# Output projection of a hybrid encoder layer: seven half-size products in two passes instead of one full product, on one Trainium2 core

## The chip, the cores and the metric

The kernel runs on one core of one Trainium2 chip. The metric is the device time in microseconds of one execution; the median of a few runs is compared. A profiled execution of the same program gives the trace from which all rows below come. In those rows PE is TensorE (the matrix engine) and PEld its weight loads, DVE is VectorE, ACT is ScalarE, POOL is GpSimd, SP is SyncE, which only issues DMAs here.

## The reference

One layer on 512 tokens of width 1024, all in float32. Two branches mix the tokens and a gated FFN follows:

```python
h = rmsnorm(x, mix_norm)
p = h @ w_in                                   # 1024 x 9248
rx, ry, qkv, z, ba, gates = split(p)
y_rnn = rglru_branch(rx, ry, ...) @ w_rnn_proj # 1536 x 1024
y_dn = deltanet_branch(qkv, z, ba, ...) @ w_dn_proj
g_rnn, g_dn = split(sigmoid(gates))
x = x + (g_rnn * y_rnn + g_dn * y_dn) @ w_out  # 1024 x 1024: the output projection
h = rmsnorm(x, ffn_norm)
gt, up = split(h @ w_gate_up)                  # 1024 x 5632
x = x + (silu(gt) * up) @ w_down               # 2816 x 1024
return rmsnorm(x, final_norm)
```

DeltaNet has 8 heads of width 128, worked on here as four pairs of heads.

## The kernel before, in words

**Matmuls in three terms.** Float32 operands are split into a rounded part (`hi`) and the rest (`lo = raw - f(hi)`). Each product is `hi*hi + hi*lo + lo*hi`, three matmuls. ScalarE makes `hi` (a cast), VectorE makes `lo` (a subtraction); `parts_of`, `split` and `stage` do this.

**Weights.** SP loads them block by block into a ring of four buffers `wraw` of 128 x 1024 floats; a buffer is free again when ScalarE and VectorE have split it. `stage` and `weights` put the parts into `whi` and `wlo`, others into tiles of the pools `t2` (128 x 512) and `t4` (128 x 1024), which all show as `t` in the profile.

**Order.** The program is first recorded: each operation goes into a list with its engine, the tiles it touches, a cost and a due time. `Plan.order()` then lays out one order for each engine from costs, due times and the free buffers, and that order is what is built; at run time each engine, and SP's queue too, takes its instructions strictly in that order and waits for semaphores. `spend(us)` opens a new recording stage, and the table `TIMES` gives each stage the due time at which its operations are sorted. All instructions are issued in one helper, so the rows all have line L384; tiles tell them apart.

**Stages.** First norm; the RG-LRU branch and the input projection; then the four head pairs `g` of DeltaNet: `dn_mats`, `dn_inverse` (a triangular inverse by small dependent steps on VectorE), `dn_state` and `dn_out`, with input projections and gates between them that keep TensorE at work. Then `dn_part(h0, nh, n)` does DeltaNet's projection for column block `n` over `nh` heads, first heads 0 to 5 and then 6 and 7, and adds the gated result to `mixs`, the mixed sum, transposed (features on partitions, tokens along the free dimension), as four tiles of two feature blocks.

**Output projection (`out_mm`).** `mixs` is split into `mh`. The 512 tokens are four blocks `c` of 128, kept as rows `x1[c]` (in the tile `na`). For the first half of the columns the four weight blocks `k2` (256 rows x 512 columns) are run over all four `c`, into four PSUM banks; for the second half each `c` is done alone with all weights ready (`weights_w`). Each `c` is added to `x1[c]`, squared, scaled by its norm, and, two blocks at a time, transposed and split by `norm_split` into `hh2` and `hl2`, first the tokens 0 to 255, then 256 to 511. The unsplit transposes stay in `a1` (tokens 0 to 255) and `a2`.

**Gate/up and down.** Two tiles `n` are done plainly (`gate_up_plain`), by token halves through `mm3`. The other twenty already use seven products for eight on blocks 2 x 2 (`gate_up`): VectorE forms four sums of the weights, and the combinations `q5`, `q7`, `q6`, `q3` of `a1` and `a2` are made once. `m` is the first combination that VectorE reads from the `st` bank of a tile. The down projection does the same in two passes; its weight sums are made ahead by `down_sums` (two additions on VectorE for each of eleven blocks, stored to DRAM as `sums`), which stands behind the last split of `mixs`.

Of the kernel before, what the change touches and what calls it, by code (L numbers as in the profile page):

```python
# [14 lines left out]
P = 128  # L15
# [39 lines left out]
LASTK = 3  # L55
GATES = (0, 2, 4, 6, 16)
# [333 lines left out]
def trunk(ctx: ExitStack, tc: tile.TileContext, x, mix_norm, w_in, rg_conv_w, rg_conv_b, rg_wa, rg_ba, rg_wx, rg_bx,  # L390
# [789 lines left out]

    gates = [(rnn_gate, n) for n in range(KD)] + [(dn_gate, n) for n in range(KD)]
    for g in range(4):
        spend()
        dn_mats(g)
        spend()
        dn_inverse(g)
        spend()
        dn_state(g)
        if g < 3:
            dn_z(g)  # L1190
        spend()
        dn_out(g)
        if g < 3:
            dn_front(g + 1)
        if g == 2:
            dn_z(3)
        for fn, n in gates[GATES[g]:GATES[g + 1]]:
            fn(n)
    spend()
    for h in range(6):  # L1200
        dn_split(h)
    for n in range(KD):
        dn_part(0, 6, n)
    spend()
    for h in (6, 7):
        dn_split(h)
    mh = []
    for n in range(KD):
        dn_part(6, 2, n)
        y = four(F32R)  # L1210
        split(mixs[n // 2][:, n % 2, :], y)
        mh.append(y)
# [10 lines left out]
    scaled = {}  # L1223

    def norm_split(c0, whole):


        sc = [scaled[c] for c in (c0, c0 + 1)]
        for k2 in range(KD // 2):
            pt = axb()  # L1230
# [11 lines left out]
    def weights_w(src):  # L1242
        now = plan.t
        raw = new(wp, (P, 2, 512), "wraw", NW)
        hi = four(F32R)
        lo = four(F32R)
        plan.t = now - 20
        Q.dma_start(raw, src)
        plan.t = now - AHEAD
        A.copy(hi, raw)  # L1250
        V.tensor_tensor(lo, raw, f(hi), ALU.subtract)
        plan.t = now
        return hi, lo

    wo = w_out[0].rearrange("(k p) n -> p k n", p=P)
    hh2 = new(hp, (P, KD, S), "hh", 1, F32R)
    hl2 = new(hp, (P, KD, S), "hl", 1, F32R)
    def out_mm(po, c, k2, hi, lo):
        spend(1.3)
        cs_ = slice(c * P, (c + 1) * P)  # L1260
        for k in (2 * k2, 2 * k2 + 1):
            T.matmul(po, mh[k][:, 0, cs_], hi[:, k % 2, :], start=k == 0, stop=False)
            T.matmul(po, mh[k][:, 0, cs_], lo[:, k % 2, :], start=False, stop=False)
            T.matmul(po, mh[k][:, 1, cs_], hi[:, k % 2, :], start=False, stop=k == KD - 1)

    def wo_part(k2, half):
        return wo[:, 2 * k2:2 * k2 + 2, half * 512:(half + 1) * 512]
# [6 lines left out]
    ssh = []  # L1274
    for c in range(NT):
        V.tensor_tensor(x1[c][:, 0:512], pos[c], x1[c][:, 0:512], ALU.add)
        sa = small([P, 1], "ssq", 4)
        A.activation(two(), x1[c][:, 0:512], AF.Square, accum_out=sa)
        sb = small([P, 1], "ssh", 4)
        V.tensor_scalar(sb, sa, 1.0 / D, EPS, ALU.mult, ALU.add)  # L1280
        ssh.append(sb)
    ws = [weights_w(wo_part(k2, 1)) for k2 in range(4)]
    a1 = [four(shape=(P, 4, 256)) for _ in range(2)]
    a2 = [four(shape=(P, 4, 256)) for _ in range(2)]
    for c in range(NT):
        po = mmb()
        for k2 in range(4):
            out_mm(po, c, k2, *ws[k2])
        V.tensor_tensor(x1[c][:, 512:D], po, x1[c][:, 512:D], ALU.add)
        plan.t -= 10  # L1290
        scaled[c] = four(shape=(P, D))
        ssq, rst, rin = (small([P, 1], t, 4) for t in ("ssq", "rst", "rin"))
        V.scalar_tensor_tensor(two(), x1[c][:, 512:D], 1.0, x1[c][:, 512:D], ALU.mult, ALU.mult, accum_out=ssq)
        act(rst, ssq, AF.Sqrt, scale=1.0 / D, bias=ssh[c])
        V.reciprocal(rin, rst)
        V.tensor_scalar(scaled[c], x1[c], rin, None, ALU.mult)
        plan.t += 10
        if c % 2:
            norm_split(c - 1, a1 if c == 1 else a2)

# [13 lines left out]
    def gate_up_plain(n):  # L1314
        pos = []
        for c0 in (n * P, D_FF + n * P):
# [3 lines left out]
            mm3(po, hi, lo, lambda k: hh2[:, k, :], lambda k: hl2[:, k, :], KD, 2)  # L1320
# [3 lines left out]
        for h in range(2):  # L1324
# [304 lines left out]
```

## Time and profile before

| | |
|---|---|
| median of three runs | 1057.54 us (1056.54 to 1057.62) |
| the profiled execution | 1057.59 us, its span in the trace 1055.8 us |
| TensorE's granted clock, mean | 0.998 |
| instructions | 17690 |
| bytes moved by DMA | 122.83 MB |

The page gives, for each engine, its busy time, the share of the span and the count; for the chain that ended last, the share of each engine; and groups of instructions as `out<-in shapes xcount | busy us, mean ns of one | idle before`. A table of stages has one row for each stretch of the span: its length, then the busy time and the count of each engine, the granted clock, the mean busy share of the 16 DMA engines and GB/s. A row of the timeline has start, duration, engine, operation, and in brackets the idle time just before with what ended it.

### The profile page before, as it was taken

How to read it: one execution, taken by the hardware profiler on the slowest of the kernel's cores; microseconds unless marked ns; L12 is line 12 of the kernel's file. 1: busy time of each engine (PE TensorE's matmuls, PEld its weight loads, DVE VectorE, ACT ScalarE, POOL GpSimd, SP SyncE). 2: the span in 40 equal slices, each digit the busy share in tenths (PEclk: the TensorE clock that was granted, in tenths of full speed). 3: DMA queues.
4: the chain of work that ended last, by engine and by line, in shares of the span. 5: the costliest groups of instructions: out<-in, count | busy, mean ns of one | idle time of the engine just before them, and what ended most of it. 6: DMA issues, size and time to landing. Idle time of an engine off the chain costs nothing.

```text
span 1055.8 us, 17690 instructions
## 1 busy us (share of the span) xinstructions
PE 1042.7 (99%) x6731; PEld 909.3 (86%) x6731; DVE 868.2 (82%) x1606; ACT 676.9 (64%) x1245; POOL 61.4 (6%) x109
## 2 busy tenths in 40 slices
PE   8999999999999999999999999999999999999997
PEld 7888888888888888888888798789999999998886
DVE  7669999659895797489479558879999988889997
ACT  7799989596538678675766643447554453546664
POOL 2000000105100321000020000000000000000000
PEclk9999999999999999999999999999999999999999
DMA  9422232224441243313202223875554333336532
GB/s 271 110 70 80 81 95 75 85 80 125 117 118 52 58 117 100 91 43 98 72 25 78 79 71 123 300 238 177 170 183 148 101 105 96 100 115 214 192 119 80
DMA packets 174389, 122.83 MB, mean 116 GB/s; under 512 B 5952, under 2 KB 160720, under 8 KB 174304
## 3 DMA queue, kind: packets, MB, share of 16 engines
q1 hardware_dynamic: 172832, 118.41, 37.3%
q10 hardware_dynamic: 1184, 3.15, 0.8%
q8 instruction: 53, 0.87, 0.3%
q14 instruction: 32, 0.26, 0.1%
q0 software_dynamic: 288, 0.13, 0.1%
HBM read 113.78 MB, written 7.90 MB: 115 GB/s over the span
## 4 chain that ended last, share of the span: by engine, by line
PE 96%; DMA 1%; ACT 1%; DVE 1%; issue 0%; ACTq 0%; SPq 0%; DVEq 0%
PE mm L384 57%; PE ax L384 24%; PE st L384 15%; ACT t L384 1%; DMA wraw<-in_w_in_dram 1%; DMA wraw<-in_w_out_dram 1%; DVE na L384 0%; DVE t L384 0%; DVE wlo L384 0%; ACTq L384 0%; ACT L384 0%; ACT rst L384 0%; SPq L384 0%; ACT hh L384 0%; DVE hl L384 0%
## 5 line engine op out<-in xcount | busy, mean ns | idle before, releaser
L384 DVE TENSOR_TENSOR t<-t,t 128x512 fp32r<-128x512 f32 (+22 forms) x489 | 242.9, 506 | 29.6 <-ACT t L384 18.5
L384 PE MATMUL mm<-hh,whi 128*128 128x512 f32 (+2 forms) x648 | 228.8, 363 | 0.0
L384 PE MATMUL mm<-hl,whi 128*128 128x512 f32 (+2 forms) x648 | 228.4, 362 | 0.0
L384 ACT CAST whi<-wraw 128x1024 fp32r<-128x1024 f32 (+3 forms) x139 | 130.1, 937 | 128.4 <-PE mm L384 60.5
L384 DVE TENSOR_TENSOR wlo<-wraw,whi 128x1024 fp32r<-128x1024 f32 (+3 forms) x138 | 151.3, 1096 | 59.4 <-ACT whi L384 29.3
L384 PE MATMUL mm<-hh,wlo 128*128 128x512 f32 (+1 forms) x632 | 146.6, 364 | 0.0
L384 PE MATMUL ax<-t,t 32*32 32x32 f32 (+3 forms) x1062 | 138.4, 285 | 0.3 <-issue 0.3
L384 PEld LDWEIGHTS mm<-hh,whi 128*128 128x128 f32 (+1 forms) x648 | 121.6, 188 | 17.0
L384 PEld LDWEIGHTS mm<-hl,whi 128*128 128x128 f32 (+1 forms) x648 | 121.6, 188 | 16.9
L384 ACT CAST t<-t 128x512 fp32r<-128x512 f32 (+2 forms) x140 | 88.7, 650 | 56.0 <-DVE t L384 50.7
L384 PEld LDWEIGHTS ax<-t,t 128*128 128x128 f32 (+1 forms) x1062 | 109.6, 159 | 17.4 <-issue 2.1
L384 PEld LDWEIGHTS mm<-hh,wlo 128*128 128x128 f32 x632 | 108.6, 189 | 17.3 <-issue 0.2
L384 ACT ACT_TABLE_LOAD x70 | 89.8, 1283 | 4.8 <-PEq L1615 1.7
L384 DVE SCALAR_TENSOR_TENSOR t<-mm,par,t 128x511 f32<-128x511 f32 (+1 forms) x108 | 80.0, 742 | 13.0 <-ACT t L384 11.9
L384 PE MATMUL mm<-t,t 128*128 128x256 f32 (+1 forms) x468 | 89.9, 336 | 0.0
L384 PE MATMUL mm<-t,whi 128*128 128x512 f32 x320 | 81.7, 395 | 0.0
L384 PEld LDWEIGHTS mm<-t,t 128*128 128x128 f32 x468 | 72.8, 190 | 8.9 <-DVE t L384 0.2
L384 PEld LDWEIGHTS mm<-t,whi 128*128 128x128 f32 x320 | 59.3, 188 | 12.4 <-ACT whi L384 0.4
L384 ACT CAST t<-wraw 128x1024 fp32r<-128x1024 f32 (+1 forms) x51 | 44.6, 880 | 26.3 <-DMA wraw<-in_w_gate_up_dram 8.8
L384 ACT ACTIVATE t<-t 128x128 f32<-128x128 f32 (+4 forms) x86 | 46.9, 558 | 22.4 <-DVE t L384 20.9
L384 DVE TENSOR_TENSOR t<-wraw,t 128x1024 fp32r<-128x1024 f32 (+1 forms) x51 | 51.2, 1006 | 2.5 <-ACT t L384 2.4
L384 POOL TENSOR_SCALAR_AFFINE_SELECT t<-t 128x512 f32<-128x512 f32 x32 | 33.1, 1042 | 163.9 <-DMA t<-gcr 103.2
(206 smaller groups left out, 1695.0 us busy)
## 6 DMA issues: line engine op xcount, KB each, us to landing
wraw<-in_w_in_dram SPq DMA_DIRECT2D x72, 512.0 KB, 3.7
wraw<-in_w_gate_up_dram SPq DMA_DIRECT2D x44, 512.0 KB, 3.8
wraw<-in_w_rnn_proj_dram SPq DMA_DIRECT2D x16, 384.0 KB, 3.4
t<-in_w_down_dram SPq DMA_DIRECT2D x11, 512.0 KB, 7.3
sums<-t SPq DMA_DIRECT2D x11, 512.0 KB, 4.4
wraw<-sums SPq DMA_DIRECT2D x11, 512.0 KB, 3.2
wraw<-in_w_down_dram SPq DMA_DIRECT2D x22, 256.0 KB, 3.8
wraw<-in_w_down_dram SPq DMA_DIRECT2D x11, 512.0 KB, 3.6
```

The costliest lines, as they stand in the source:

```text
L384: self.plan.add(e, lambda: real(*a, **kw), outs, ins, cost, tail, table)
```

## The change

The output projection `Y = X W` is done by blocks 2 x 2: tokens in halves (the two pairs of blocks `c`), features and columns in halves. Seven products of half-size blocks, named "1" to "7", take the place of eight; each contracts over 512 features as four pairs of 128-blocks `j`. The scheme is the one that gate/up and down have.

- *Weight sums* (`out_sums`): after the second head pair (`g == 1`) is recorded, four blocks `j` of `w_out` are loaded, two buffers of `wraw` each, four additions of 512 columns make the sums, and they are stored to DRAM as `osums`.
- *DeltaNet's projection* is cut 4 and 4 heads instead of 6 and 2 (`DSPLIT`).
- *Token combinations* (`out_q`, `out_q2`): made from `mixs` as its tiles are completed; the second set is made while the first pass runs.
- *First pass*: products "6", "7", "5", "1" for both token blocks `i`, into eight PSUM banks, `j` by `j`. Then `m` is formed and added to three quarters of `x1`.
- *Second pass*: "4" goes on in the bank of "7", "2" in that of "1", "3" in that of "5". "4" completes the tokens 256 to 511, whose norm is then done first; "2" and "3" complete the tokens 0 to 255.
- `gate_up_plain` runs the second token half first. Part of the squares and of the scaling moves from VectorE to ScalarE, and half of `norm_split`'s transposes use the `st` banks.
- `TIMES` is another table throughout.

```diff
+DSPLIT = 4
-    def mm3(po, hi, lo, xh, xl, kk, parts=1):
+    def mm3(po, hi, lo, xh, xl, kk, parts=1, last_first=False):
-        for t in range(0, S, n):
+        for t in range(0, S, n)[::-1 if last_first else 1]:
...
+    wo = w_out[0].rearrange("(j h p) n -> p j h n", p=P, h=2)
+    def out_sums(j):
+        ra, rb, s_ = new(wp, (P, 2, 512), "wraw", NW), new(wp, (P, 2, 512), "wraw", NW), four()
+        Q.dma_start(ra, wo[:, j, 0, :].rearrange("p (h n) -> p h n", h=2))
+        Q.dma_start(rb, wo[:, j, 1, :].rearrange("p (h n) -> p h n", h=2))
+        V.tensor_tensor(s_[:, 0, :], ra[:, 0, :], ra[:, 1, :], ALU.add)
+        V.tensor_tensor(s_[:, 1, :], ra[:, 1, :], rb[:, 1, :], ALU.add)
+        V.tensor_tensor(rb[:, 1, :], s_[:, 0, :], rb[:, 1, :], ALU.add)
+        V.tensor_tensor(rb[:, 0, :], rb[:, 1, :], rb[:, 0, :], ALU.add)
+        Q.dma_start(osums[j][:, 0], s_)
+        Q.dma_start(osums[j][:, 1], rb)
...
-    for h in range(6):
+    for h in range(DSPLIT):
         dn_split(h)
     for n in range(KD):
-        dn_part(0, 6, n)
+        dn_part(0, DSPLIT, n)
...
+    def out_q(j):
+        mj = mixs[j].rearrange("p h (s t) -> p (h s) t", s=2)
+        q = two(shape=(P, 2, 256))
+        V.tensor_tensor(q, mj[:, 0:2, :], mj[:, 1:4:2, :], ALU.subtract)
+        V.tensor_tensor(mj[:, 1, :], mj[:, 0, :], q[:, 1, :], ALU.subtract)
+        (p1, p6), (p7, p5) = pair(mj[:, 0:2, :], 2), pair(q, 2)
+    def out_q2(j):
+        V.tensor_tensor(mj[:, 1, :], mj[:, 2, :], mj[:, 1, :], ALU.subtract)
+        p3, p2, p4 = pair(mj[:, 1:4, :], 3)
...
-    pos = [stb(), stb(), axb(), axb()]
-    for k2 in range(4):
-        hi, lo = stage(lambda raw: [(raw, wo_part(k2, 0))], (P, 2, 512))
-        for c in range(NT):
-            out_mm(pos[c], c, k2, hi, lo)
+    def out_w(j):
+        Q.dma_start(ra[:, 0, :], wo[:, j, 0, 0:512])
+        Q.dma_start(ra[:, 1, :], osums[j][:, 1, 1, :])
+        Q.dma_start(rs, osums[j][:, 0])
+        (w1, w6), (w5, w7) = halves(ra, True), halves(rs)
+    def out_w2(j):
+        Q.dma_start(r, wo[:, j, 1, :].rearrange("p (h n) -> p h n", h=2))
+        Q.dma_start(t4_, osums[j][:, 1, 0, :])
+        w2, w3 = halves(r)
+        parts_of(t4_, th, tl, 0)
+    ob = {"6": [stb(), stb()], "7": [axb(), axb()], "5": [axb(), mmb()], "1": [mmb(), mmb()]}
+    for j in range(nj):
+        spend(5.5)
+        w4 = out_w(j)
+        for name in "6751":
+            for i in range(2):
+                half_mm(ob[name][i], i, w4[name], xq[j][name], j == 0, j == nj - 1)
+        out_q2(j)
...
+    for i in range(2):
+        V.tensor_tensor(hi_[:, 512:D], hi_[:, 512:D], ob["7"][i], ALU.subtract)
+        V.tensor_tensor(hi_[:, 512:D], hi_[:, 512:D], ob["5"][i], ALU.add)
+        V.tensor_tensor(m, ob["6"][i], m, ALU.subtract)
+        V.tensor_tensor(hi_[:, 0:512], hi_[:, 0:512], m, ALU.subtract)
+        V.tensor_tensor(hi_[:, 512:D], hi_[:, 512:D], m, ALU.add)
+        V.tensor_tensor(lo_[:, 512:D], lo_[:, 512:D], m, ALU.add)
...
+    for j in range(nj):
+        w3s.append(out_w2(j))
+    def out_last(name, bank, i):
+        for j in range(nj):
+            half_mm(ob[bank][i], i, w3s[j][name], xq[j][name], False, j == nj - 1, True)
+    for i in range(2):
+        out_last("4", "7", i)
+        sc.append(scale_chunk(2 + i, 0, False))
+    norm_split(2, sc, a2)
+    for i in range(2):
+        out_last("2", "1", i)
+    for i in range(2):
+        out_last("3", "5", i)
+        sc.append(scale_chunk(i, 512, True))
+    norm_split(0, sc, a1)
...
 TIMES = [
-    -193727, -159384, -193730, -126073, -120235, -159028, -125968, -63810, -13198, -66391, -64154, -63637, -49334,
+    -176998, -159417, -176656, -106634, -96501, -159195, -96162, -70221, 191167, -94063, -87550, -69365, -34065,
```

What the new order is at three places. TensorE, in the middle of the output projection. Before, at the turn from the first half of the columns to the second: `st_1137` is the bank of the last token block of the first half, `mm_1186` that of the second block of the second half.

```order
L384 MATMUL st_1137<-whi_1150,t_1129 128x512
L384 MATMUL st_1137<-wlo_1151,t_1129 128x512
...
L384 MATMUL mm_1186<-t_1165,t_1087 128x512
L384 MATMUL mm_1186<-t_1166,t_1087 128x512
...
L384 MATMUL mm_1186<-t_1165,t_1093 128x512
L384 MATMUL mm_1186<-t_1166,t_1093 128x512
```

Now, at the turn from the first pass to the second: `mm_1171` is a bank of "1", `ax_1168` one of "5" (product "3" goes on in it), `ax_1166` the bank of "7" for `i = 0`, in which "4" goes on; `t_1178`, `t_1186` and `t_1194` are the combinations of `out_q2` for `j` = 0, 1 and 2.

```order
L384 MATMUL mm_1171<-whi_1198,t_1154 128x512
L384 MATMUL mm_1171<-wlo_1199,t_1154 128x512
L384 MATMUL ax_1168<-t_1218,t_1178 128x512
L384 MATMUL ax_1168<-t_1219,t_1178 128x512
L384 MATMUL ax_1168<-t_1218,t_1179 128x512
L384 MATMUL mm_1171<-whi_1198,t_1155 128x512
L384 MATMUL ax_1166<-t_1220,t_1178 128x512
L384 MATMUL ax_1166<-t_1221,t_1178 128x512
L384 MATMUL ax_1166<-t_1220,t_1179 128x512
L384 MATMUL ax_1166<-t_1226,t_1186 128x512
```

What moved: a matmul of product "3" already stands among the last ones of the first pass, and the second pass begins with "4", whose weight sums come from `osums`.

VectorE, in the second half of the same stage. Before, around the additions of the first half (`na` is `x1`); `t_1317`, `t_1341` and `t_1366` are blocks of `down_sums`, `wlo_1215` and `wlo_1219` weights of the first plain gate/up tile.

```order
L384 TENSOR_TENSOR t_1317<-t_1317 128x512
L384 TENSOR_TENSOR na_1130<-mm_1180,na_1130 128x512
L384 TENSOR_TENSOR na_1130<-ax_1139,na_1130 128x512
...
L384 TENSOR_TENSOR wlo_1215<-wraw_1213,whi_1214 128x1024
...
L384 TENSOR_TENSOR t_1341<-t_1341 128x512
L384 TENSOR_TENSOR wlo_1219<-wraw_1217,whi_1218 128x1024
...
L384 TENSOR_TENSOR t_1366<-t_1366 128x512
```

Now, around the splits of the second pass's weights: `t_1225`, `t_1231` and `t_1237` are the `lo` parts for products "2" and "3" of `j` = 1, 2 and 3; `t_1305`, `t_1330`, `t_1354`, `t_1403` and `t_1379` are blocks of `down_sums`.

```order
L384 TENSOR_TENSOR t_1225<-wraw_1222,t_1224 128x1024
L384 TENSOR_TENSOR t_1305<-t_1305 128x512
L384 TENSOR_TENSOR t_1330<-t_1330 128x512
...
L384 TENSOR_TENSOR t_1305<-t_1305,t_1306 128x512
L384 TENSOR_TENSOR t_1231<-wraw_1228,t_1230 128x1024
L384 TENSOR_TENSOR t_1330<-t_1330,t_1331 128x512
L384 TENSOR_TENSOR t_1354<-t_1354 128x512
L384 TENSOR_TENSOR t_1403<-t_1403 128x512
L384 TENSOR_TENSOR t_1354<-t_1354,t_1355 128x512
L384 TENSOR_TENSOR t_1237<-wraw_1234,t_1236 128x1024
```

What moved: sums for the down stage, seven additions of 512 columns here, stand between the splits that the second pass waits for. Of the 22 additions of `down_sums`, 12 stood ahead of the first `m` before and the rest within the next six gate/up tiles; now 10 stand ahead of it and the rest reach to the twelfth tile.

SP's queue, for the same time. Before, weights of the output projection (`in_w_out_dram`) between loads and stores of `down_sums`:

```order
L384 DMA wraw_1167<-in_w_out_dram 128x2x512
L384 DMA t_1292<-in_w_down_dram 128x1024
L384 DMA t_1293<-in_w_down_dram 128x512
L384 DMA wraw_1170<-in_w_out_dram 128x2x512
L384 DMA sums_1245<-t_1243 128x1024
L384 DMA wraw_1173<-in_w_out_dram 128x2x512
```

Now, the weights of the second pass: `wraw_1216` to `wraw_1234` are those of products "2" and "3" for `j` = 0 to 3.

```order
L384 DMA t_1235<-osums_814 128x512
L384 DMA wraw_1216<-in_w_out_dram 128x1024
L384 DMA t_1306<-in_w_down_dram 128x512
L384 DMA t_1331<-in_w_down_dram 128x512
L384 DMA t_1305<-in_w_down_dram 128x1024
L384 DMA t_1330<-in_w_down_dram 128x1024
L384 DMA wraw_1222<-in_w_out_dram 128x1024
L384 DMA t_1354<-in_w_down_dram 128x1024
L384 DMA t_1355<-in_w_down_dram 128x512
L384 DMA wraw_1228<-in_w_out_dram 128x1024
L384 DMA wraw_1234<-in_w_out_dram 128x1024
```

What moved: four loads of `w_down` blocks now stand between the first and the second block of the second pass's weights, and two more ahead of the third.

More of the change, by code (lines that the diff above doesn't have):

```diff
@@ L1198, in trunk, with pair @@
             fn(n)
+        if g == 1:
+            for j in range(KD // 2):
+                out_sums(j)
     spend()
-    for h in range(6):
+    for h in range(DSPLIT):
         dn_split(h)
     for n in range(KD):
-        dn_part(0, 6, n)
+        dn_part(0, DSPLIT, n)
     spend()
-    for h in (6, 7):
+    for h in range(DSPLIT, H):
         dn_split(h)
-    mh = []
+    xq = {}
+    def pair(src, n):
+        hi, lo = (four if n > 2 else two)(F32R, (P, n, 256)), (four if n > 2 else two)(F32R, (P, n, 256))
+        parts_of(src, hi, lo, 0)
+        return [(hi[:, i, :], lo[:, i, :]) for i in range(n)]
+    def out_q(j):
[4 more added lines that the diff above has]
+        (p1, p6), (p7, p5) = pair(mj[:, 0:2, :], 2), pair(q, 2)
+        xq[j] = {"1": p1, "6": p6, "7": p7, "5": p5}
+    def out_q2(j):
+        mj = mixs[j].rearrange("p h (s t) -> p (h s) t", s=2)
+        V.tensor_tensor(mj[:, 1, :], mj[:, 2, :], mj[:, 1, :], ALU.subtract)
+        p3, p2, p4 = pair(mj[:, 1:4, :], 3)
+        xq[j].update({"3": p3, "2": p2, "4": p4})
     for n in range(KD):
[L1209 to L1212, printed above, removed]
+        dn_part(DSPLIT, H - DSPLIT, n)
+        if n % 2:
+            out_q(n // 2)
     last_split = (len(plan.ops) - 1,)
@@ L1282, in trunk, with half_mm, halves @@
-    ws = [weights_w(wo_part(k2, 1)) for k2 in range(4)]
+    def half_mm(po, i, w, x_, start, stop, add=False):
+        (wh, wl), (xh, xl) = w, x_
+        cs_ = slice(i * P, (i + 1) * P)
+        T.matmul(po, xh[:, cs_], wh, start=start, stop=False, skip_group_check=add)
+        T.matmul(po, xh[:, cs_], wl, start=False, stop=False, skip_group_check=add)
+        T.matmul(po, xl[:, cs_], wh, start=False, stop=stop, skip_group_check=add)
+    def halves(src, own=False):
+        hi, lo = (new(wp, (P, 2, 512), t, 2, F32R) if own else four(F32R) for t in ("whi", "wlo"))
+        parts_of(src, hi, lo, 0)
+        return [(hi[:, i, :], lo[:, i, :]) for i in range(2)]
@@ L1283, in trunk @@
     a1 = [four(shape=(P, 4, 256)) for _ in range(2)]
     a2 = [four(shape=(P, 4, 256)) for _ in range(2)]
[L1285 to L1291, printed above, removed]
-        ssq, rst, rin = (small([P, 1], t, 4) for t in ("ssq", "rst", "rin"))
-        V.scalar_tensor_tensor(two(), x1[c][:, 512:D], 1.0, x1[c][:, 512:D], ALU.mult, ALU.mult, accum_out=ssq)
+    w3s = []
@@ new lines, in trunk, with scale_chunk @@
+    for j in range(nj):
+        spend(0.1)
+        w3s.append(out_w2(j))
+    def out_last(name, bank, i):
+        spend(2.7)
+        for j in range(nj):
+            half_mm(ob[bank][i], i, w3s[j][name], xq[j][name], False, j == nj - 1, True)
+    def scale_chunk(c, n0, late):
+        ssq, rst, rin = (small([P, 1], t, 4) for t in ("ssq", "rst", "rin"))
+        sc = four(shape=(P, D))
+        xv = x1[c][:, n0:n0 + 512]
+        if late:
+            V.scalar_tensor_tensor(two(), xv, 1.0, xv, ALU.mult, ALU.mult, accum_out=ssq)
+        else:
+            A.activation(two(), xv, AF.Square, accum_out=ssq)
@@ L1323, in gate_up_plain @@
         act(s_, pos[0], AF.Silu)
-        for h in range(2):
+        for h in (1, 0):
             o = 256 * (h ^ n % 2)
```

86 lines of the change are left out of this document (48 added, 38 removed), and 27 rows, old and new, of the table TIMES.

## The prediction

> **What bounds the kernel now.** I read the page first, then the waits of TensorE, then the chain in order of time, then a table of stages.
>
> ```profile
> span 1055.8 us, 17690 instructions
> ...
> PE 1042.7 (99%) x6731; PEld 909.3 (86%) x6731; DVE 868.2 (82%) x1606; ACT 676.9 (64%) x1245; POOL 61.4 (6%) x109
> ...
> PE 96%; DMA 1%; ACT 1%; DVE 1%; issue 0%; ACTq 0%; SPq 0%; DVEq 0%
> ```
>
> TensorE is busy for 99% of the span and makes up 96% of the chain that ended last. Since a busy share of pipelined matmuls can hide small waits, the next view lists every wait of TensorE: six rows, 5.8 us in all, and all but one of the longer ones stand at the start of the program.
>
> ```profile
> PE ax L384 <- DMA gain1r<-in_mix_norm_dram: 2.9, 1, 2.9
> PE mm L384 <- DVE hl L384: 1.4, 2, 0.9
> PE ax L384 <- ACT t L384: 0.5, 1, 0.5
> PE ax L384 <- DVE t L384: 0.5, 1, 0.5
> PE ax L384 <- issue: 0.3, 1, 0.3
> PE mm L384 <- ACT t L384: 0.2, 1, 0.2
> ```
>
> So the time is the number of matmuls times their pace. The chain in order of time gives the pace where nothing else runs: 41.93 / 185 = 0.2266 us for a matmul of 512 columns, and 1.44 / 12 = 0.120 us for one of 256.
>
> ```profile
> 277.00 41.93 PE mm L384 x185
> ...
> 743.41 1.44 PE st L384 x12
> ```
>
> The third view cuts the second half of the span into stages: the end of the DeltaNet work, its output projection's start, the output projection proper with the second norm (655 to 735), then the gate/up stage in two parts, and the down stage.
>
> ```profile
> core 0: us, PE busy (x) PEld busy (x) DVE busy (x) ACT busy (x) POOL busy (x), PEclk, DMA share, GB/s
> 300.00:625.00 325.00, 324.69 (x2550) 275.21 (x2549) 235.57 (x595) 215.29 (x482) 30.99 (x58) 1.00 0.26 73
> 625.00:655.00 30.00, 30.00 (x144) 25.00 (x142) 23.46 (x44) 13.04 (x25) 0.00 (x0) 1.00 0.41 136
> 655.00:735.00 80.00, 79.49 (x428) 67.62 (x427) 67.46 (x107) 42.25 (x74) 0.00 (x0) 1.00 0.74 240
> 735.00:800.00 65.00, 65.00 (x544) 65.00 (x543) 64.97 (x115) 34.05 (x60) 0.00 (x0) 1.00 0.54 175
> 800.00:925.00 125.00, 125.00 (x1044) 125.00 (x1043) 109.70 (x196) 59.56 (x109) 0.00 (x0) 1.00 0.35 104
> ```
>
> TensorE is full in every stage. VectorE is second: 67.46 of 80 us in the stage that changes, and full (64.97 of 65) right after it. That is where the change can be paid for.
>
> **The change, part by part.** The sum is made against the profiled execution, 1057.59 us (its span is 1055.8, the rest lies around it), against a median of 1057.54.
>
> *Matmuls.* Before, the output projection is 2 column halves x 4 token blocks x 8 row blocks x 3 terms = 192 matmuls of 512 columns. After, it is 7 products x 2 token blocks x 4 pairs x 3 terms = 168. All other matmuls keep their number and width (DeltaNet's projection in 4 and 4 heads for 6 and 2 too). 24 x 0.2266 = 5.44 us go, all on the path that sets the end: minus 5.44.
>
> *Vector work.* The price of an operation is the distance between starts, since they overlap:
>
> ```profile
> 671.83 0.69 DVE L384 TENSOR_TENSOR t<-t 128x512 f32<-128x512 f32 x1
> 672.55 1.89 DVE L384 TENSOR_TENSOR t<-t,t 128x512 f32<-128x512 f32 x3
> ...
> 728.65 1.22 DVE L384 TENSOR_TENSOR t<-t,t 128x1024 f32<-128x1024 f32 x1
> 729.79 0.68 DVE L384 TENSOR_TENSOR hl<-t,hh 128x512 fp32r<-128x512 f32 x1
> 730.39 2.35 DVE L384 TENSOR_TENSOR t<-t,t 128x1024 fp32r<-128x1024 f32 x2
> ...
> 684.37 0.42 DVE L384 TENSOR_TENSOR wlo<-wraw,whi 128x256 fp32r<-128x256 f32 x1
> ...
> 734.93 0.74 DVE L384 TENSOR_TENSOR t<-t,mm 128x256 f32<-128x256 f32 x2
> ```
>
> Three of 512 columns take 1.89 us and one 0.69, so the next starts (1.89 - 0.69) / 2 = 0.60 us later; for 1024 columns 2.35 - 1.22 = 1.13. For 256 it is 0.74 - 0.42 = 0.32; for 768 I take 0.87, between 512 and 1024. The page "VectorE: DVE Perf Modes" of the Trainium skill says, under "The DRAIN you can't avoid", that the next operation does not start until the pipe is empty; by that rule the price would be the whole 0.69 and 1.22, and these rows do not bear it out.
>
> Counted in the order, the change adds 16 sums of weights in the DeltaNet stages (16 x 0.60 = 9.6 us). In the output projection it adds 18 operations of 512 columns (10.8), 8 of 256 (2.6), 4 of 1024 (4.5) and 4 of 768 (3.5) and loses about 3 us, since part of squaring and scaling goes to ScalarE: 18.4 us. Both together are 28.0 us on an engine that is not the bound.
>
> *Does it fit under the matmuls?* DeltaNet first: VectorE is busy for 235.57 of 325 us there, so 89 us are free for 9.6. But two of the four block pairs of sums stand between the small steps of the triangular inverse, which run one after the other on VectorE, so the cost lies between 0 and 9.6 us. I take 0, as TensorE was busy for 324.69 us of that stage with projections that fill those steps.
>
> For the output stage I count, in both orders, from the multiply that reads the first product of the DeltaNet projection's second part (after its first part in the order of before) to the first `m` of the gate/up stage. Before: 82 operations of 512, 22 of 1024, 12 of 256, 3 of 768 and some 6 us of others are 86.6 us of vector work, beside 323 matmuls of 512, 216 of 256 and 32 transposes (about 0.11 us each) = 102.6 us. After: 101, 26, 13 and 4, with 2.5 us of others, are 100.3 us, beside 300, 270 and 32 = 103.9 us. The room falls from 16.0 us to 3.6. It still fits, but VectorE must be kept fed for the whole stretch. In before some of its idle time there was forced:
>
> ```profile
> 670.08 1.23 DVE L384 TENSOR_TENSOR t<-wraw,t 128x1024 fp32r<-128x1024 f32 x1 [1.44 <-ACT t L384]
> ...
> 672.61 0.50 PE L384 MATMUL ax<-whi,t 128*128 128x512 f32 x1 [0.51 <-ACT t L384]
> ...
> 689.68 0.69 DVE L384 TENSOR_TENSOR t<-mm,t 128x512 f32<-128x512 f32 x1 [4.89 <-PE mm L384]
> ```
>
> The first row is a real shortage (weights that landed late, and TensorE then waited 0.51 us, in the second row). The third is the opposite: VectorE was ahead and waited for TensorE. Between none of the 16.0 us forced (cost 0) and all of it (16.0 - 3.6 = 12.4 us), I take 1 us, near the first row, which is the only one of the stretch that reached TensorE.
>
> *Transfers.* The new sums are 8 reads and 8 writes of the queue in the DeltaNet stages, where the DMA share is 0.26, and they take slots of the four `wraw` buffers. What stands behind a store that waits for VectorE on SP's queue is the next weights of the input projection.
>
> ```profile
> sums<-t SPq DMA_DIRECT2D x11, 512.0 KB, 4.4
> ```
>
> A store of this kind lands in 4.4 us, one slot's hold: 0 to 4.4 us, taken 0, since such stores already stand in the gate/up stage, where TensorE is busy 65.00 of 65 us. In the output stage the reads grow from 8 x 512 KB to 4 x 1792 KB, 3.1 MB more. Before, 80 us x 240 GB/s = 19.2 MB were moved there; 22.3 MB in 74.6 us would be 299 GB/s. The page has the rate of each slice:
>
> ```profile
> GB/s 271 110 70 80 81 95 75 85 80 125 117 118 52 58 117 100 91 43 98 72 25 78 79 71 123 300 238 177 170 183 148 101 105 96 100 115 214 192 119 80
> ```
>
> At the 300 GB/s of its best slice the bytes take 74.3 us (cost 0), at the 271 of the first slice, which waits for its inputs alone, 82.3 us (7.7 too many). I take 0: the loads for the down stage can go later, where the table shows 175 and 104 GB/s.
>
> *ScalarE* gets a dozen casts, some copies and six scalings, and loses four of its table loads, 5.1 us:
>
> ```profile
> L384 ACT ACT_TABLE_LOAD x70 | 89.8, 1283 | 4.8 <-PEq L1615 1.7
> ```
>
> With 42.25 of 80 us busy it hides the rest. The second token half first only exchanges which half of the norm is finished last. In before that tail runs from the last addition to the first `hl` of its half, 725.71 - 717.75 = 8.0 us:
>
> ```profile
> 717.75 0.69 DVE L384 TENSOR_TENSOR na<-mm,na 128x512 f32<-128x512 f32 x1
> ...
> 725.71 0.69 DVE L384 TENSOR_TENSOR hl<-t,hh 128x512 fp32r<-128x512 f32 x1
> ```
>
> It is covered, before and after, by the two plain gate/up tiles on the other half, 4 x 24 matmuls x 0.120 = 11.5 us. Cost 0; without that cover, 8.0.
>
> Sum: 1057.59 - 5.44 + 1.0 = 1053.15, said as 1053.2 us, 0.4% less. What a measurement of this kernel tells from no change is about 0.2%, 2.1 us.
>
> **The rivals.** *Everything fits (0.10).* No wait is added and the 0.51 us goes: 1057.59 - 5.44 - 0.51 = 1051.6 us. For it: the waits of TensorE above are tiny after the start. Against: 3.6 us of room.
>
> *The vector engine does not fit (0.11, slower).* Place: from the last DeltaNet projection to the first gate/up tiles. If the idle time of before was mostly forced by waits on ScalarE and DMA, TensorE waits up to 12.4 us: 1057.59 - 5.44 + 12.4 = 1064.6. It decides from 5.4 + 2.1 = 7.5 us of waits on, that is when more than 3.6 + 7.5 = 11 of the 16 us were forced. Against it: 4.89 us of them are one wait for TensorE; behind the stretch, 735 to 800, VectorE is full with TensorE not waiting at all. The Trainium skill's rule on draining ("VectorE: DVE Perf Modes"), named above, would make the vector work of the stretch some 113 us against 103.9 and give this rival; the overlapped starts speak against it.
>
> *Loads bind the second pass (0.14).* The four late blocks of weights stand in SP's queue between loads for the down stage, and VectorE's queue has sums of those loads ahead of the last split. Half of the 7.7 us, 3.9, on top of the forecast: 1053.15 + 3.9 = 1057.0 us, so no difference to be measured; a third of it is still faster, all of it slower. For it: the DMA share of 0.74 and the late weights at 670. Against: only 0.51 us came of that.
>
> *A cold TensorE (0.03).* If one wait at the turn between the passes grows to 3 us, the matmuls after it may run at half pace. The start of the program shows such a pace after an idle stretch:
>
> ```profile
> 3.09 4.41 PE L384 MATMUL ax<-ones 128*128 128x128 f32 x20
> ...
> 8.35 1.20 PE L384 MATMUL ax<-ident,t 128*128 128x128 f32 x9 [0.46 <-DVE t L384]
> ```
>
> Twenty matmuls in 4.41 us are 0.22 us each; nine later ones in 1.20 are 0.13 with the tail. So a wait of 3 us would cost 3 + 2.2: 1057.59 - 5.44 + 5.2 = 1057.4 us. The Trainium skill's "TensorE: Matmul & The Clock Gate", Part 1, says that an idle window of about 3.4 us halves the clock until the engine has been busy as long again; the start agrees in its pace, and no wait later in this trace is long enough to show it.
>
> **How the numbers follow.** The forecast (small waits of 0 to 2.5 us: 1052.2 to 1054.7) has 0.62. It, the full fit (0.10) and a part of the load case (0.04) are faster by more than 0.2%: 0.76. The rest of the load case and the cold engine (0.13), and the vector case where it stays small (0.02), are within 0.2%: 0.15. The vector case otherwise is slower: 0.09. The range goes from 0.2 us below the full fit to the load case and the cold engine, 1051.4 to 1057.4; what it leaves out is the vector case and the ends of the others.
>
> **What would show it.** Right: 24 matmuls fewer at 0.2266 us, VectorE's busy time up by some 28 us, waits of TensorE between 640 and 740 us of 1 to 2 us, and VectorE full from the last DeltaNet projection until well into gate/up. Wrong: rows of TensorE waiting for `wlo` or `t` of VectorE of several us (the vector case), ScalarE's casts waiting for output weights or `osums` (the load case), a granted clock below 1.00, or new idle time of TensorE in the inverse at the second head pair (the DeltaNet sums on the chain).

## The result, and the profile after

The changed kernel took 1054.62 us (median of 11 runs, 1052.77 to 1055.38) against 1056.91 us (11 runs, 1055.68 to 1057.62) of the kernel before, measured with it: a ratio of 0.9975, 95% interval 0.9966 to 0.9985. That is 2.3 us less by the medians, 0.25% by the ratio. The forecast was 1053.2 us and 4.4 us less. The profiled execution took 1052.97 us; it is one of the shortest of its eleven, and the profiled one of before, 1057.59 us, is as long as the longest of its kernel, so their difference of 4.6 us flatters the change.

The page of after, engines:

```profile
span 1051.1 us, 17768 instructions
...
PE 1037.1 (99%) x6707; PEld 905.0 (86%) x6707; DVE 891.1 (85%) x1650; ACT 689.5 (66%) x1265; POOL 54.4 (5%) x109
```

Twenty-four matmuls are gone (6731 to 6707) and VectorE has 22.9 us more (868.2 to 891.1). The waits of TensorE in after:

```profile
PE ax L384 <- DVE ident L384: 2.6, 1, 2.6
PE ax L384 <- issue: 1.6, 1, 1.6
PE mm L384 <- DVE hl L384: 1.3, 2, 0.8
PE mm L384 <- DVE t L384: 1.2, 1, 1.2
PE ax L384 <- DVE t L384: 0.6, 3, 0.3
PE st L384 <- ACT hh L384: 0.2, 1, 0.2
```

Rows one and three stand at the start, as before; of row five 0.27 us does, the rest stands at 320 us (0.22) and 638 us (0.16). The last row stands at 714 us. New are 1.6 us of "issue" (the engine waits for nothing that the profile shows; 0.3 before) and 1.2 us for VectorE's `t`. The table of stages, cut as before, tells where they are:

```profile
core 0: us, PE busy (x) PEld busy (x) DVE busy (x) ACT busy (x) POOL busy (x), PEclk, DMA share, GB/s
300.00:625.00 325.00, 321.93 (x2528) 272.88 (x2527) 243.75 (x602) 204.46 (x467) 30.68 (x58) 1.00 0.34 99
625.00:655.00 30.00, 29.84 (x155) 24.76 (x154) 24.48 (x58) 14.44 (x35) 0.00 (x0) 1.00 0.39 127
655.00:735.00 80.00, 79.76 (x446) 69.09 (x445) 78.58 (x124) 57.21 (x96) 0.00 (x0) 1.00 0.74 253
735.00:800.00 65.00, 65.00 (x541) 64.81 (x541) 64.51 (x111) 34.17 (x61) 0.00 (x0) 1.00 0.49 149
800.00:925.00 125.00, 125.00 (x1043) 124.96 (x1043) 116.77 (x210) 61.47 (x109) 0.00 (x0) 1.00 0.44 138
```

The output projection (655 to 735) is what was feared for, and it is clean: VectorE is busy 78.58 of 80 us there, DMA at 253 GB/s, and TensorE 79.76 (79.49 before). The loss is in the DeltaNet stages, where the change only adds the sums of weights: 325.00 - 321.93 = 3.07 us of idle TensorE, 0.31 before. Two places make up 2.77 us of it. The first is at 391 us, all engines in order of time:

```profile
388.00 2.88 PE L384 MATMUL mm<-t,whi 128*128 128x512 f32 x12
388.20 0.78 ACT L384 ACTIVATE t<-mm,zero_t,par 128x512 f32<-128x512 f32 x1 [0.97 <-PE mm L384]
389.78 0.95 DVE L384 TENSOR_TENSOR wlo<-wraw,whi 128x768 fp32r<-128x768 f32 x1
...
390.85 0.74 DVE L384 SCALAR_TENSOR_TENSOR t<-mm,par,t 128x510 f32<-128x510 f32 x1
...
391.70 0.75 DVE L384 SCALAR_TENSOR_TENSOR t<-mm,par,t 128x511 f32<-128x511 f32 x1
...
392.55 0.75 DVE L384 SCALAR_TENSOR_TENSOR t<-mm,par,t 128x511 f32<-128x511 f32 x1
...
393.44 2.74 PE L384 MATMUL mm<-t,whi 128*128 128x512 f32 x11 [1.20 <-DVE t L384]
...
399.97 0.60 ACT L384 ACTIVATE t<-mm 128x512 f32<-128x512 f32 x1
```

A convolution reads its PSUM bank `mm` with one ScalarE step (ready at 388.98) and three multiply-adds on VectorE. These are queued behind a weight split and between small steps of the triangular inverse, so the bank is free only at 393.30, and the next matmuls of the RG-LRU projection, which need a bank, come 1.20 us late. VectorE was hardly earlier before. The same place there, where TensorE goes on at 392.19 without a wait:

```profile
383.51 0.60 ACT L384 ACTIVATE t<-mm 128x512 f32<-128x512 f32 x1
...
388.11 2.88 PE L384 MATMUL mm<-t,whi 128*128 128x512 f32 x12
388.31 0.78 ACT L384 ACTIVATE t<-mm,zero_t,par 128x512 f32<-128x512 f32 x1 [0.97 <-PE mm L384]
...
391.48 0.74 DVE L384 SCALAR_TENSOR_TENSOR t<-mm,par,t 128x511 f32<-128x511 f32 x1
...
392.19 2.88 PE L384 MATMUL mm<-t,whi 128*128 128x512 f32 x12
392.32 0.74 DVE L384 SCALAR_TENSOR_TENSOR t<-mm,par,t 128x511 f32<-128x511 f32 x1
```

There the third multiply-add ended at 393.06, but TensorE's next product did not need its bank. The program has three `mm` banks. Before, the next product went into the bank that ScalarE had read at 383.51. In the new order that third bank holds another product, which ScalarE reads only at 399.97, so the next product has to go into the bank of the convolution. What is new is the use of the banks, and VectorE's late read now shows.

The sums of output weights are not near: the first of them runs at 400.8. The second place is in the inverse of the third head pair; TensorE alone, of after:

```profile
503.26 0.75 PE L384 MATMUL ax<-t,na 32*32 32x32 f32 x64
...
505.53 0.95 PE L384 MATMUL ax<-t,t 32*32 32x32 f32 x89
508.06 0.26 PE L384 MATMUL ax<-t,t 32*32 32x32 f32 x7 [1.57 <-issue]
```

A group of 96 small matmuls runs as far as its 89th; then TensorE stands still for 1.57 us with no wait in the records. The same place in before, where 0.26 us were lost behind the 79th:

```profile
504.69 0.75 PE L384 MATMUL ax<-t,na 32*32 32x32 f32 x64
...
506.96 0.87 PE L384 MATMUL ax<-t,t 32*32 32x32 f32 x79
508.09 0.32 PE L384 MATMUL ax<-t,t 32*32 32x32 f32 x17 [0.26 <-issue]
```

Counted from the program's start it is the same place in TensorE's program: 6081 of its instructions in the trace stand ahead of it in after, 6082 in before. That suggested the fetch of its program: the page lists the queue that carries it, and 0.85 MB in 52 transfers for 2 x 6707 instructions are 16 KB and about 256 instructions each.

```profile
q8 instruction: 52, 0.85, 0.3%
```

### The profile page after: what moved, and what is told of

It is laid out like the page before. It is cut to its first block, busy times and chain, and to the rows that moved or that the text cites. A ratio compares the mean times of both kernels' runs of the same rounds, so it can differ in the third digit from the quotient of the medians.

```text
span 1051.1 us, 17768 instructions
## 1 busy us (share of the span) xinstructions
PE 1037.1 (99%) x6707; PEld 905.0 (86%) x6707; DVE 891.1 (85%) x1650; ACT 689.5 (66%) x1265; POOL 54.4 (5%) x109
## 4 chain that ended last, share of the span: by engine, by line
PE 91%; DVE 5%; ACT 2%; issue 1%; DMA 1%; ACTq 0%; SPq 0%; DVEq 0%
PE mm L384 53%; PE ax L384 23%; PE st L384 15%; DVE t L384 3%; DVE na L384 1%; ACT t L384 1%; DVE wlo L384 1%; DMA wraw<-in_w_in_dram 1%; ACT hh L384 0%; ACTq L384 0%; ACT L384 0%; ACT whi L384 0%; SPq L384 0%; DVE so L384 0%; DVE hl L384 0%
## 5 line engine op out<-in xcount | busy, mean ns | idle before, releaser
L384 DVE TENSOR_TENSOR t<-t,t 128x512 fp32r<-128x512 f32 (+26 forms) x501 | 249.4, 512 | 24.1 <-ACT t L384 15.8
L384 DVE TENSOR_TENSOR wlo<-wraw,whi 128x1024 fp32r<-128x1024 f32 (+2 forms) x138 | 150.6, 1092 | 40.8 <-ACT whi L384 19.6
L384 PE MATMUL ax<-t,t 128*128 128x512 f32 (+3 forms) x1134 | 156.9, 291 | 1.6 <-issue 1.6
L384 PEld LDWEIGHTS ax<-t,t 128*128 128x128 f32 (+1 forms) x1134 | 123.1, 161 | 21.5 <-issue 3.5
L384 ACT CAST t<-t 128x512 fp32r<-128x512 f32 (+2 forms) x148 | 94.9, 654 | 43.7 <-DVE t L384 33.9
L384 PE MATMUL mm<-t,t 128*128 128x256 f32 (+1 forms) x420 | 80.3, 330 | 0.0
L384 PEld LDWEIGHTS mm<-t,t 128*128 128x128 f32 x420 | 63.8, 190 | 6.6
L384 ACT CAST t<-wraw 128x1024 fp32r<-128x1024 f32 (+1 forms) x55 | 49.2, 896 | 23.3 <-DMA wraw<-in_w_gate_up_dram 14.5
L384 DVE TENSOR_TENSOR t<-wraw,t 128x1024 fp32r<-128x1024 f32 (+1 forms) x55 | 56.6, 1032 | 1.1 <-ACT t L384 0.7
L384 PE MATMUL mm<-t,wlo 128*128 128x512 f32 x160 | 42.9, 394 | 0.0
```

The source lines that it names most:

```text
L384: self.plan.add(e, lambda: real(*a, **kw), outs, ins, cost, tail, table)
```

## The experiments

Theory A: the matmuls are worth their 5.4 us, the output stage costs nothing, and what is missing went into these two waits, which came with the new order. Theory B: VectorE's additional work costs the time. All kernels below keep the order of their base unless the edit says so; where a step is thinned or left out, only what is built in its place changes.

**The base again, and 24 matmuls alone.** First the changed kernel unchanged.

> The changed kernel once more, for a second trace and as the base of this set. Theory A (the 24 matmuls are worth 5.4 us, and what is missing of it went into new waits of TensorE in the DeltaNet stages, 1.20 us at 391.9 and 1.57 us at 506.5 in the first trace): both waits stand in the new trace at the same instructions, and the time is about 1054.6 us, 2.3 under the kernel before. Theory B (VectorE's 28 us of additional work cost time): waits of TensorE for VectorE between 625 and 800 us.

It took 1054.50 us against 1056.70 (ratio 0.9976, 0.9967 to 0.9984), with waits of 1.16 us and 1.94 us at the same two places: not an accident of one execution. Then before, with matmuls left out (`leave` holds for `k2` = 1 and 2 in the first half of the columns and for `k2` = 1 in the second; 24 of the 64 third terms, which is three eighths):

```diff
             T.matmul(po, mh[k][:, 1, cs_], hi[:, k % 2, :], start=False, stop=k == KD - 1)
+            if leave:
+                instead(lambda: None)
```

> The kernel before with 24 of the 192 matmuls of its output projection left out (the third term of a quarter of the row blocks), order and everything else kept. Theory A: 24 x 0.2266 = 5.4 us less than before, about 1051.5 us. If a matmul removed is worth less than its pace (theory C, the freed time turns into waits at once), about 1054.6, as the changed kernel.

It took 1052.93 us (0.9967, 0.9955 to 0.9979): 3.8 us less, between the two theories. Part of what is missing shows in its trace, at two matmuls that read weights:

```profile
678.63 0.74 PE L384 MATMUL st<-whi,t 128*128 128x512 f32 x2 [0.24 <-ACT whi L384]
...
681.27 0.50 PE L384 MATMUL st<-wlo,t 128*128 128x512 f32 x1 [0.73 <-DVE wlo L384]
```

With the matmuls gone and all splits kept, TensorE ran ahead of the splits: 0.97 us of new waits, while the 0.51 us of before at 672 are gone. The rest of the missing 1.7 us was not found. So a matmul removed is worth its pace only where its neighbours keep up. That they do in the changed kernel is argued from its waits in the output stage, which come to 0.24 us.

**The output stage without 20 us of VectorE's work.** Every `lo` of the output projection is made one column wide, and the matmuls read `hi` in its place:

```diff
         parts_of(src, hi, lo, 0)
+        instead(lambda: nc.vector.tensor_tensor(lo[:, 0, 0:1], src[:, 0, 0:1], f(hi[:, 0, 0:1]), ALU.subtract))
...
         T.matmul(po, xh[:, cs_], wl, start=False, stop=False, skip_group_check=add)
+        instead(lambda: nc.tensor.matmul(po, xh[:, cs_], wh, start=False, stop=False, skip_group_check=add))
```

> The changed kernel with the lo parts of the output projection's operands not made (one column each; the matmuls read hi in their place, as many as before): 4 x (1.20 + 0.87 + 2.26 + 1.73) = 24 us of VectorE work less between 640 and 720 us, more than the 18.4 that the change added there; order kept. Theory A: TensorE does not wait there, so at most 0.5 us faster than the changed kernel. Theory B: 2 to 5 us faster.

1054.65 us, against 1054.50 with the work: nothing. The page has 870.5 us of VectorE's busy time for 890.6, so 20 us were taken out, not the 24 of the estimate; that is still more than the 18.4 in question. Theory B falls for the output stage.

**The sums of weights in DeltaNet.** All 16 sums one column wide; so that no store reads what is not written, the first store of each block reads `rb` instead of `s_`.

```diff
         V.tensor_tensor(s_[:, 0, :], ra[:, 0, :], ra[:, 1, :], ALU.add)
+        instead(lambda: nc.vector.tensor_tensor(s_[:, 0, 0:1], ra[:, 0, 0:1], ra[:, 1, 0:1], ALU.add))
...
         Q.dma_start(osums[j][:, 0], s_)
+        instead(lambda: nc.sync.dma_start(osums[j][:, 0], rb))
```

> The changed kernel with its 16 sums of output weights in the DeltaNet stages one column wide instead of 512, stores and loads and order kept: 9.6 us of VectorE work less there. Theory A: no difference to the changed kernel (1054.6 us, within 0.5), as these sums stand after the first of the two waits and hide under the projections. Theory B: 1 to 3 us faster, and one of the two waits gone.

It took 1062.70 us, 8 us longer with 8.8 us of VectorE's busy time less (890.6 to 881.8). The edit had made a wait of its own; VectorE's rows, then TensorE's:

```profile
412.04 0.16 DVE L1204 TENSOR_TENSOR wraw<-wraw 128x1 f32<-128x1 f32 x1 [6.47 <-DMA osums<-wraw]
...
421.25 0.21 DVE L1204 TENSOR_TENSOR wraw<-wraw 128x1 f32<-128x1 f32 x1 [3.30 <-DMA osums<-wraw]
...
444.75 0.16 DVE L1204 TENSOR_TENSOR wraw<-wraw 128x1 f32<-128x1 f32 x1 [6.12 <-DMA osums<-wraw]
```

```profile
423.01 0.50 PE L384 MATMUL mm<-hh,whi 128*128 128x512 f32 x1 [2.30 <-ACT whi L384]
...
445.23 1.80 PE L384 MATMUL st<-t,na 128*128 128x128 f32 x8 [2.88 <-DVE t L384]
```

The fourth sum writes into `rb` and now had to wait until the store out of `rb` had landed. It says nothing on the price of the sums, but that a wait of 6 us in VectorE's queue comes through to TensorE in these stages. So once more, with only the third and fourth sum thin and the stores as they were:

> The changed kernel with the third and fourth sum of each block of output weights one column wide (8 of the 16, so 8 x 0.54 = 4.3 us of VectorE work less in the DeltaNet stages); stores, loads and order kept, and no store reads what a later sum writes. Theory A: as the changed kernel, 1054.5 us within 0.5. Theory B (the sums cost time): 1 to 2 us faster.

1055.24 us (0.9983, 0.9974 to 0.9992): no faster, but 0.7 us longer than 1054.50, more than the 0.5 that was allowed. Six of its eleven executions have a mean clock of 0.996 or 0.997, against two of eleven in the base; the five others (1053.2 to 1054.5 us) lie among those of the base. So the 4.3 us of sums show no price, and one of some tenths of a microsecond cannot be excluded. The other two sums of each block were not tried on their own; no wait of TensorE stands at them in any trace of the changed kernel.

**The two waits taken away.** First the border of the instruction blocks. A float32 matmul is two weight loads and two matmuls in the trace, so TensorE gets 26 x 4 instructions more in its idle time at the start and 3 x 4 less, which moves every later border by 92 instructions:

```diff
         T.matmul(idle[:, 0:P], ones, ones, start=True, stop=True)
+        if i == 0:
+            def more():
+                for _ in range(26):
+                    nc.tensor.matmul(idle[0:32, 0:32], ones[0:32, 0:32], ones[0:32, 0:32], start=True, stop=True)
+                nc.tensor.matmul(idle[:, 0:P], ones, ones, start=True, stop=True)
+            instead(more)
+        elif i > 6:
+            instead(lambda: None)
```

> The changed kernel with 26 small matmuls of 32 columns put into TensorE's idle time at the start and 3 of the ten warm-up matmuls left out: 92 more instructions on TensorE ahead of everything, nothing else moved. Theory A2 (the idle time of 1.57 to 1.94 us behind 506 us is the fetch of TensorE's instructions, which come in blocks of 256: the block's border stands 16 instructions before the end of a dense group of small matmuls): the border moves 92 instructions forward, between the two dense groups, and the idle time goes; 1.6 to 1.9 us less idle time in the trace, and 1 to 3 us off the time (1054.5 to about 1052.5), since a clock of half speed behind it goes too where it came. Rival (a wait of the data, a semaphore that the trace does not show): idle time as before, 1054.5 us.

The 96 now run through, and 1053.48 us (0.9966, 0.9956 to 0.9977) are 1.0 less than 1054.50 (the intervals of the two ratios overlap, so alone this gain is not clear of noise):

```profile
506.49 1.02 PE L384 MATMUL ax<-t,t 32*32 32x32 f32 x96
507.44 1.88 PE L384 MATMUL mm<-hh,wlo 128*128 128x512 f32 x7
```

Some of it came back: a wait of 0.16 us for the last DeltaNet heads at 638 is now 0.65. The control moves the borders by one whole block, with 67 small matmuls in place of 26:

> The changed kernel with 67 small matmuls instead of 26 at the start and 3 warm-up matmuls left out: 256 more instructions on TensorE, one whole block, so that the borders of the blocks stand where they stand in the changed kernel. Theory A2: the idle time of 1.6 to 2.0 us at the same matmuls behind 506 us (plus what the start takes longer) is back. Rival (the small matmuls at the start helped in another way): it stays away. The time itself says little here, since the start becomes some 4 us longer by the 41 further small matmuls.

One execution, 1059.16 us with its longer start; the idle time is back at the same matmul:

```profile
510.59 0.95 PE L384 MATMUL ax<-t,t 32*32 32x32 f32 x89
513.57 0.26 PE L384 MATMUL ax<-t,t 32*32 32x32 f32 x7 [2.03 <-issue]
```

So it is the place of the borders that matters: moved by 92 instructions the idle time is gone, moved by a whole block it is back. Counted in the traces, the border moved otherwise than expected. In after two borders, 256 instructions apart, fall into the stretch of the two dense groups, at 503.52 and 508.06 us. With 92 more instructions only one falls there, at 506.86: it stands inside the group of 96, not between the groups, and TensorE does not stop at it. The transfer of 16 KB that preceded it began at 496.27 us; in after it began at 505.80. And the kernel before with the 92 instructions:

> The kernel before with the same 92 instructions more at the start as in the run that took the idle time from the changed kernel. Its own idle time at that place is 0.26 to 0.38 us. Theory A2: at most 0.4 us off, 1056.5 to 1056.9 us. Rival (the small matmuls help any kernel): 1 to 2 us off.

1056.48 against 1056.66 us (0.9996, 0.9987 to 1.0005): the edit does nothing for the kernel before. Next VectorE's order at 391 us, with names added to the recorded operations so that they can be found (`stt` are the three multiply-adds that read the bank `mm681`, `low` is the weight split, `small` the steps of the inverse between them):

```diff
         todo = plan.order()
+        dve = [i for i in todo if plan.ops[i][0] == "DVE"]
+        stt = [i for i in dve if "mm681" in plan.names[i][2]]
+        low = [i for i in dve if plan.names[i][1] == ["wlo452"]]
...
+        for after_, moved in ((low[0], small[0:2]), (stt[0], small[2:3]), (stt[1], small[3:4]), (stt[2], small[4:])):
+            for i in reversed(moved):
+                todo.remove(i)
+                todo.insert(todo.index(after_) + 1, i)
```

> The changed kernel with VectorE's order altered at one place: the three multiply-adds of the convolution that free the bank for which TensorE waits 1.20 us at 391.9 stand ahead of five small steps of the triangular inverse, and the weight split ahead of two; nothing else moved. Theory A: that wait goes, 1.2 us less, about 1053.3 us, unless the small steps are then late for another matmul. Rival (the freed time is lost at the next wait): the wait gone and the same 1054.5 us.

The wait is gone, and the median is 1054.07 us (0.9971, 0.9961 to 0.9980), 0.4 less and not 1.2, a difference that is not clear of noise. Its trace shows why the other wait costs more than its length; TensorE's rows, and its row for 508.0 to 511.4 in a table of stages:

```profile
507.72 0.33 PE L384 MATMUL ax<-t,t 32*32 32x32 f32 x7 [1.98 <-issue]
507.97 3.18 PE L384 MATMUL mm<-hh,wlo 128*128 128x512 f32 x7
```

```profile
508.00:511.40 3.40, 3.40 (x12) 2.72 (x10) 0.00 (x0) 3.20 (x10) 0.00 (x0) 0.59 0.02 5
```

The granted clock is 0.59 there, and seven matmuls take 3.18 us instead of the 1.88 above: 1.30 us more. In the seven traces with an idle time of 1.57 to 2.03 us at this place, three have such a stretch behind it (this one, the one without `lo` and the one with half of the sums thin) and four have not. Of the nine executions of this kernel, the five with a mean clock of 0.996 or 0.997 took 1054.1 to 1054.9 us, the four with 0.998 or 0.999 took 1052.0 to 1052.9. So five of nine had the long stretch here, by this sign; of the 22 executions of the changed kernel five have a mean clock of 0.997 or less. Both edits together:

> Both edits of this set together. Theory A with A2: 2.8 us less than the changed kernel, about 1051.7 us, which is the 5.4 us of the matmuls less small waits. Rival: no more than one of the two.

1051.56 us (0.9952, 0.9939 to 0.9964), and once more:

> The changed kernel with the border moved and the bank freed earlier, once more, as the base of this set: 1051.6 us within 0.5, 5.3 us under the kernel before.

1051.39 us (0.9951, 0.9938 to 0.9963): 5.3 us under before, as near to the 5.44 of the matmuls as the interval (3.9 to 6.5 us) can tell. This version beats both kernels. The row for the DeltaNet stages, from the first of the two runs:

```profile
300.00:625.00 325.00, 324.77 (x2544) 275.48 (x2543) 246.31 (x614) 205.32 (x471) 30.59 (x58) 1.00 0.35 100
```

324.77 of 325 us, as before. What is left to see is a wait of 1.07 us at 637 (0.82 in the second run). A last edit put matmuls ahead of it:

```diff
+        first = [i for i in todo if plan.names[i][:2] == ("PE", ["mm989"])][:8]
+        turns = [i for i in todo if plan.names[i][:2] == ("PE", ["ax926"])]
+        for i in first:
+            if todo.index(i) > todo.index(turns[0]):
+                todo.remove(i)
+                todo.insert(todo.index(turns[0]), i)
```

> The same with TensorE's order altered at a third place: seven matmuls of DeltaNet's projection, whose operands are ready, stand ahead of the transposes for which TensorE waits 1.07 us at 637 us. Theory A: that wait goes, 0.5 to 1.1 us less, about 1050.8 us. Rival: the transposed values are then late for VectorE or for the projection's second part, and the time stays at 1051.6 us.

1051.61 us: the rival was right. The wait at 637 is gone and 0.61 us stand six microseconds later, for VectorE's `t`; that it comes late since the transposes do is argued, not shown.

```profile
644.36 0.73 PE L384 MATMUL mm<-t,whi 128*128 128x512 f32 x2 [0.61 <-DVE t L384]
```

## Why the prediction was right, and where it was not

Direction and range were right; the size was 4.4 us forecast and 2.3 measured. That the time of 1054.62 us still lies within the forecast with its small waits (1052.2 to 1054.7) is partly luck: the waits came in other stages, by another mechanism, and the base was 0.7 us too high. By its steps:

- *Matmuls, -5.44.* Right in count and, with both waits gone, near in worth: 5.3 us, all small differences included. Alone, in the kernel before, 24 matmuls gave 3.8 us.
- *VectorE, +28.0 of work.* It measured 22.9, of which 243.75 - 235.57 = 8.2 lie in the DeltaNet stages (forecast 9.6) and 78.58 - 67.46 = 11.1 in the output stage (forecast 18.4). Another 116.77 - 109.70 = 7.1 stand between 800 and 925 us, where later sums of the down stage now run.
- *Waits in the output stage, +1.0.* Too much; at most 0.2 us there (80.00 - 79.76 = 0.24, where before lost 0.51 to late weights). The count that left VectorE 3.6 us of room and full engines agrees with 80.00 - 78.58 = 1.4 us of idle VectorE there, and 20 us of work taken out changed nothing. The rival in which VectorE does not fit is thereby refuted, and with it the price by the whole duration. The prediction had named that price from the Trainium skill's "VectorE: DVE Perf Modes" ("The DRAIN you can't avoid"); the same paragraph also says that a next operation which is not held starts earlier, and the starts 0.60 us apart at durations of 0.69 agree with that.
- *Sums in DeltaNet, 0.* No price was seen at half of them. The last sign of being wrong, new idle time of TensorE in the inverse at the second head pair, did appear: the 1.20 us at 391 stand there. Its cause was not the sums, which begin at 400.8. *Transfers, 0.* Right: 253 GB/s and no wait for a load there, so the rival of the late loads fell too. *ScalarE and the norm's tail, 0.* Right: ScalarE 12.6 us more (676.9 to 689.5), and of the norm's tail one wait of 0.24 us.
- *What failed* is the step that took TensorE's 324.69 of 325 us in the DeltaNet stages as cover for everything there. It costed what the change adds to these stages, not that its table of due times lays all their instructions out anew. Old instructions in a new order cost 1.20 us (the next product needs the bank that VectorE still reads, as the third one is held) and 1.57 - 0.26 = 1.3 us (a block border in a dense group). With 0.5 for the late weights that are gone, 0.6 for three small waits that before has not (at 320, 638 and 714), and the half clock, 1.3 us in five of 22 executions, so 0.3: -5.44 + 1.2 + 1.3 - 0.5 + 0.6 + 0.3 = -2.5, against -2.3 measured. The match is closer than the terms are: the second trace has 1.94 for the 1.57, and the profiled executions of the two kernels differ by 4.6 us, not 2.3. Shown is that most of the loss hangs on these two waits, since both edits together bring 3.1 us back. That the change of `TIMES` moved them is argued; no run changed that table alone.
- *The rival of a cold TensorE (0.03)* was set at the wrong place and with too long a wait: not at the turn between the passes after 3 us, but at 506 us after 1.7 to 2.0, and it cost 1.3 us there, not 2.2.
- *The base.* The sum was made against 1057.59 us, 0.7 above the later median; a forecast as a difference loses nothing by that, one as a time does.

## What to carry to other kernels

When a planner or a table lays the order out anew, compare the order in the stages that the change does not mean, too: on an engine that is 99% busy, two places of 1 to 2 us are half of a gain of 5 us. A gain in matmuls is best checked by taking away, one by one, each wait that is new in the list of waits. And an experiment that thins work must leave every store and its buffer as they were, or it measures its own wait.

## What was not expected of the hardware

- TensorE's program comes in blocks (52 transfers of 16 KB). At one place two borders of blocks fall into about 3 us of dense small matmuls. There the engine stood idle at the second border for 1.57 to 2.03 us in every trace of that order, for 0.26 and 0.38 in two traces of the order of before, and not at all when 92 more instructions left only one border in the stretch. In the last head pair one border stands in such a group in after too (at 599.59 us), and TensorE does not stop. In all nine traces with the idle time a transfer of 16 KB began 2.3 to 2.6 us before TensorE went on: at 505.69 us in before and at 505.80 in after, and both went on at 508.1. In the new order TensorE was through with its block 1.3 us earlier (506.48 for 507.83); why the transfer does not begin earlier too is open.
- An idle time of under 2 us, behind a group of small matmuls, halved the clock for 3.4 us in three of seven traces. In the trace with all sums thin the same followed the wait of 2.88 us at 445 (granted clock 0.51 from 445.6 to 449.1), with no small matmuls ahead of it. "TensorE: Matmul & The Clock Gate" of the Trainium skill, Part 1, speaks of an idle window of about 3.4 us and of a window that runs freely; that it comes in one execution and not in the next agrees with the second, the length of the idle time does not agree with the first.
